# Attention with eight heads: the last head's projection weights fetched during the fourth head, from ScalarE's queue

## The chip, the cores and the metric

The kernel runs on one core of a Trainium2 chip. The metric is the device time of one launch in microseconds (us). Before the change it is 1582.3 us, the median of three runs (1581.09 to 1584.79). One further execution was taken with the hardware profiler; every row of the trace below is from it.

The engines are named as in the profile: PE is TensorE (matmuls; PEld its weight loads), DVE is VectorE, ACT is ScalarE, POOL is GpSimd, SP is SyncE, which does nothing but issue DMAs. SPq and ACTq are the rows in which SyncE and ScalarE issue one.

## The reference, cut to what matters

The reference is a whole decoder block. An RMS-normalised input feeds a state-space branch and an attention branch; both are gated and merged, and a cross-attention and a feed-forward layer follow. The change lies in the attention branch, which computes for each of 8 heads of width 64, over 1024 tokens:

```python
q, k, v = u @ w_in[:, 512:1024], u @ w_in[:, 1024:1536], u @ w_in[:, 1536:2048]
s = einsum('bhqd,bhkd->bhqk', q, k) * 64 ** -0.5 + cum[..., :, None] - cum[..., None, :]
p = softmax(where(causal, s, -inf))
out = einsum('bhqk,bhkd->bhqd', p, v)          # cum: running sum of log sigmoid(forget logit)
```

Of `w_in`, one head's projection needs 64 columns for q and 64 for k, 1024 rows each. The GLU that is spoken of below is the product of the state-space branch with `w_glu`; its first products are made beside the last head.

## The kernel before, in words

**Precision.** Every float32 operand of a matmul is split in two: ScalarE copies a rounded "hi" part (L178, in `split`), VectorE subtracts to get "lo" (L179). A product is three matmuls, hi·hi, hi·lo, lo·hi (L168, L169, L170, in `mm3`). A block of weights therefore passes through a DMA into a `raw` tile, a copy on ScalarE into `whi`, and a subtraction on VectorE into `wlo`.

**Slots.** The pool `wpool` gives `raw`, `whi` and `wlo` four slots each, and these are shared: by the value weights, the eight heads' projection weights, the GLU's weights (`wload`, L153, two DMAs of 256 KB for each block) and later ones.

**The heads.** `Fox.run` goes through the heads h = 0 to 7. A head has 12 units (query half, key tile), numbered 0 to 11. A unit computes a tile of scores (L1650, L1651 on TensorE), adds a causal mask where the tile lies on the diagonal (L1653, VectorE), takes the exponential (L1657, ScalarE; the instruction is kept as `self.exp`), splits it (L1662 and L1663, or L1659 and L1660), and products with the values follow one or two units later (L1675, L1676, L1682).

Between the units stand pieces of other heads' work, in lists by unit (`side[i]`), so that TensorE always has something to do:

- the projection of head h+2, matmul by matmul (`parts`), with its copies out of PSUM into the `hb` tiles (`evac`, L1592 to L1598);
- the row maxima of head h+1 (L1623 on TensorE, L1625 and L1628 on VectorE). `max_row` turns them (L1637, L1639) and sends them by DMA into row 68 of that head's queries (L1640). The first scores of head h+1 read that row;
- the split of the weights of head h+3 at unit 9 (`parted`, which calls `split`), placed behind the exponential of that unit;
- the load of the weights of head h+3 at unit 5 for h = 1 to 4 (`load`, L1570 and L1571): two DMAs of 256 KB in rows of 256 bytes, issued by SyncE, and placed behind `self.spread`, the DMA that spreads the row of reciprocal sums of head h−1 (L1697, in `finish`).

So the weights of head 7 are loaded and split in head 4. `finish` sends a row of sums away, inverts it (L1694, VectorE) and fetches it back spread over 64 partitions (L1693, L1695, L1697); `divide` multiplies by it after unit 4 of the next head, splits the result and stores it (L1703, L178, L179, L1709). `gate_rows` fetches two rows of decay sums into the `hb` tiles (L1605, L1606).

**What sets the order.** The source above gives priorities; a scheduler in the compiler orders each engine's instructions and places the waits. `behind(ins)` and `issue_after(ins)` add a tie: the instructions inside stand behind `ins` on its engine, without a semaphore. In the trace, instructions can therefore stand earlier than in the source: the GLU's loads, which are written in head 7 (`filler`), are issued by SyncE in head 4, and their splits follow the split of head 7's weights.

**Other loads on SyncE near the change.** In heads 5 and 6, `load_y` (L1728) brings 16 pieces of the state-space branch's result.

Of the kernel before, what the change touches and what calls it, by code (L numbers as in the profile page):

```python
# [24 lines left out]
NH = 8  # L25
# [24 lines left out]
C_U, C_Q, C_K, C_V, C_G = 0, 512, 1024, 1536, 2056  # L50
# [16 lines left out]
def f32(ap):  # L67
    return ap.bitcast(F32)
# [26 lines left out]
def weave(main, side, lead=0):  # L95

    n, m, done = len(main) - lead, len(side), 0
    for i, f in enumerate(main):
        f()
        want = m if i + 1 == len(main) else max(0, (i + 1 - lead) * m // max(n, 1))  # L100
        while done < want:
            side[done]()
            done += 1
# [986 lines left out]
class Glu:  # L1090
# [6 lines left out]
    def load(self, j):  # L1097
        pieces = [(512 * i, (4, P), self.w_glu[:, :, i * D + j * P:i * D + (j + 1) * P].rearrange("k p c -> p k c"))
                  for i in range(2)]
        self.w[j] = [t[:, :D].rearrange("p (k c) -> p k c", k=8) for t in self.B.wload(pieces, D)]  # L1100
# [348 lines left out]
class Fox:  # L1449
# [109 lines left out]
    def project(self, h):  # L1559

        B = self.B
        V, A, S = B.V, B.A, B.S
        K1, K2, Q1, Q2 = self.hb[h % 2]

        def load(behind=None):
            src = lambda c: self.w_in[:, c + h * DH:c + (h + 1) * DH].rearrange("(k p) c -> p k c", p=P)
            raw = self.raw[h] = B.wpool.tile([P, RAW], F32, tag="raw", bufs=4, name="raw")[:, :D]
            rv = raw.rearrange("p (k c) -> p k c", k=8)
            with B.behind(behind):
                S.dma_start(rv[:, :, 0:64], src(C_Q))  # L1570
                return S.dma_start(rv[:, :, 64:128], src(C_K))  # L1571

        def parted(behind=None):
            wh = B.wpool.tile([P, WSLOT], F32R, tag="whi", name="whi")[:, :D]
            wl = B.wpool.tile([P, WSLOT], F32R, tag="wlo", name="wlo")[:, :D]
            with B.behind(behind):
                B.split(wh, wl, self.raw.pop(h))
            self.pj[h] = [t.rearrange("p (k c) -> p k c", k=8) for t in (wh, wl)]

        def part(hf, k):  # L1580
            if k == 0:
                self.pj[h, hf] = B.bank("mm")
            wh, wl = self.pj[h]
            rh, rl = self.uT.rhs(k, hf)
            B.mm3(self.pj[h, hf], wh[:, k, :], wl[:, k, :], rh, rl, k == 0, k == 7)

        def evac(hf):
            if hf == 1 and h > 1:
                self.gate_rows(h)
            ps = self.pj.pop((h, hf))  # L1590
            cs = slice(512 * hf, 512 * hf + 512)
            A.activation(Q1[0:64, cs], ps[0:64, :], AF.Copy, scale=0.125)  # L1592
            A.copy(K1[0:64, cs], ps[64:128, :])
            V.scalar_tensor_tensor(out=Q2[64:128, cs], in0=ps[0:64, :], scalar=0.125, in1=f32(Q1[0:64, cs]),
                                   op0=ALU.mult, op1=ALU.subtract)
            V.tensor_sub(K2[0:64, cs], ps[64:128, :], f32(K1[0:64, cs]))
            A.activation(Q2[0:64, cs], ps[0:64, :], AF.Copy, scale=0.125)
            return A.copy(K2[64:128, cs], ps[64:128, :])  # L1598

        return Projection(load, parted, [lambda hf=hf, k=k: part(hf, k) for hf in range(2) for k in range(8)],  # L1600
                          [lambda: evac(0), lambda: evac(1)])

# [113 lines left out]
    def run(self, y_d, yT, aT, w_glu, w_d, filler):  # L1716
        B, fp, S = self.B, self.fp, self.B.S
        self.aT = aT
        self.prepare_v()
        for t in range(NT):  # L1720
            self.values_of_v(1, t)
        self.log_forget()
        self.setup()

        def load_y(k, h):

            for i, dst in enumerate(yT.rhs(k, h)):
                S.dma_start(f32(dst).rearrange("p (t c) -> p t c", t=4),  # L1728
                            y_d[k, i, 4 * h:4 * h + 4].rearrange("t p c -> p t c"))

        def load_att(k):
            for h in range(2):
                for i, dst in enumerate(aT.rhs(k, h)):
                    S.dma_start(f32(dst), self.att_d[i, k * P:(k + 1) * P, 512 * h:512 * h + 512])

        pro = [self.project(h) for h in range(NH)]
        for h in range(2):
            loaded = pro[h].load()
            pro[h].split()

        with B.tc.issue_after(loaded.ins):
            for k in range(4):
                S.dma_start(w_d[k].rearrange("(m g) c -> m g c", g=8),
                            w_glu[k * P:(k + 1) * P].rearrange("(g m) c -> m g c", m=16))
        for f in pro[0].parts[:8] + pro[0].evac[:1] + pro[0].parts[8:] + pro[0].evac[1:]:
            f()
        self.cumulate()
        for t in range(4):
            self.values_of_v(0, t)
        for h in range(2):  # L1750
            self.gate_rows(h)
        for f in pro[1].parts[:4]:
            f()
        weave(pro[1].parts[4:8] + pro[1].evac[:1] + pro[1].parts[8:], self.row_max(0))
        copied = pro[1].evac[1]()
        self.values_of_v(0, 4)
        self.max_row(0)
        pro[2].load()
        pro[2].split(copied)
        pro[3].load()  # L1760
        for t in range(5, 7):
            self.values_of_v(0, t)
        units = [(qc, kt) for qc in range(2) for kt in range(4 * qc + 4)]
        for h in range(NH):
            side = {i: [] for i in range(12)}
            late = h == NH - 2
            if late:
                for i, f in enumerate(pro[h + 1].parts[8:]):
                    side[i // 2].append(f)
                side[3].append(pro[h + 1].evac[1])  # L1770
            if h + 1 < NH:
                for i, f in enumerate(self.row_max(h + 1)):
                    side[(RSLOT_LATE if late else RSLOT)[i]].append(f)
                side[9].append(lambda: self.max_row(h + 1))
            if h + 2 < NH:
                n = 8 if h + 3 == NH else 16
                for i, f in enumerate(pro[h + 2].parts[:n]):
                    side[i if n == 8 else PSLOT[i]].append(f)
                side[9].append(pro[h + 2].evac[0])
                if n == 16:  # L1780
                    side[11].append(pro[h + 2].evac[1])
            if h + 3 < NH:
                side[9].append(lambda: pro[h + 3].split(self.exp))
            if h > 0 and h + 3 < NH:
                side[5].append(lambda: pro[h + 3].load(self.spread))
            if h == 0:
                side[0].append(lambda: self.values_of_v(0, 7))
            if late:
                for k in range(8):
                    side[4 + k].append(lambda k=k: load_y(k // 2, k % 2))  # L1790
            if h == NH - 1:
                for k in range(3):
                    side[6 + k].append(lambda k=k: load_att(k))
                for i, f in enumerate(filler):
                    side[i * 12 // len(filler)].append(f)
            for i, u in enumerate(units):
                self.scores(h, *u)
                for f in side[i]:
                    f()
                if len(self.hi_todo) > 2:  # L1800
                    self.values_hi()
                if len(self.lo_todo) > 1:
                    self.values_lo()
                if h and i == 4:
                    with B.tc.issue_after(self.mark.ins):
                        self.divide(h - 1)
        while self.hi_todo:
            self.values_hi()
        while self.lo_todo:
            self.values_lo()  # L1810
        self.divide(NH - 1)
# [29 lines left out]
```

## Time and profile before

| | |
|---|---|
| median of three runs | 1582.3 us |
| the profiled execution | 1584.62 us |
| its span, first to last instruction | 1582.9 us |
| TensorE busy | 1536.4 us, 97% of the span |
| VectorE busy | 1026.6 us, 65% |
| ScalarE busy | 658.3 us, 42% |
| mean granted clock of TensorE | 0.985 of full speed |
| bytes moved by DMA | 240.87 MB, 152 GB/s over the span |

Times in rows of the trace are microseconds from the start of the span. A row of a timeline gives start, duration, engine, source line, operation, output and inputs with their shapes, and in brackets the time for which the engine was idle before it and what ended that. `x2` is two instructions merged into one row. In the view by stretches, each engine has its busy time and in parentheses the number of its instructions.

### The profile page before, as it was taken

The page shows a single profiled execution, that of the slowest core. Times are in us where ns is not written, and L with a number is a line of the kernel's source. Part 1 is how long each engine was busy: PE and PEld are TensorE (multiplying, and loading weights), DVE is VectorE, ACT ScalarE, POOL GpSimd, SP SyncE. Part 2 cuts the span into 40 slices and gives each one's busy share as a digit, 9 for nine tenths or more (in the row PEclk, how much of TensorE's full clock was granted, in tenths as well). Part 3 has the DMA queues.
Part 4 walks back from the last instruction along what each step waited for, and adds up shares of the span by engine and source line. Part 5 has one row for each costly group of instructions (what it writes and reads, how often), then busy time and mean ns, then how long its engine had stood idle before and what let it go on. Part 6 is the DMA issues. An engine that isn't in the chain of part 4 may idle for free.

```text
span 1582.9 us, 20443 instructions
## 1 busy us (share of the span) xinstructions
PE 1536.4 (97%) x7313; PEld 1264.3 (80%) x7313; DVE 1026.6 (65%) x1822; ACT 658.3 (42%) x1177; POOL 266.8 (17%) x343
## 2 busy tenths in 40 slices
PE   7899999999999899999999999999999999999997
PEld 6688888898777678878888778888888888788886
DVE  6746545444788687685555687777777775566555
ACT  6422434422566553232335564333333333344342
POOL 3026653200212124110002200100000000001001
PEclk8899999999999899999999999999999999999999
DMA  8753466422123746367412186555544543897652
GB/s 294 151 105 100 131 118 138 111 103 30 26 45 59 203 121 199 109 206 248 138 45 76 54 282 236 172 165 162 159 160 156 162 147 129 269 392 228 192 160 107
DMA packets 197942, 240.87 MB, mean 152 GB/s; under 512 B 35448, under 2 KB 126488, under 8 KB 197328
## 3 DMA queue, kind: packets, MB, share of 16 engines
q1 hardware_dynamic: 190640, 222.79, 47.7%
q10 hardware_dynamic: 7200, 16.78, 2.8%
q8 instruction: 57, 0.93, 0.2%
q14 instruction: 45, 0.37, 0.1%
HBM read 165.60 MB, written 75.86 MB: 153 GB/s over the span
## 4 chain that ended last, share of the span: by engine, by line
PE 83%; DVE 6%; DMA 5%; ACT 3%; issue 1%; POOL 1%; SPq 0%; POOLq 0%; ACTq 0%; DVEq 0%
PE mm L873 15%; PE mm L168 8%; PE mm L170 8%; PE mm L169 8%; PE pv L873 7%; PE mm L1010 4%; PE sc L873 4%; PE sc L168 3%; PE sc L169 3%; PE sc L170 3%; PE sc L1010 3%; PE pv L1010 3%; PE misc L1010 1%; DMA raw<-in_w_in_dram 1%; PE mm L1623 1%
## 5 line engine op out<-in xcount | busy, mean ns | idle before, releaser
L178 ACT CAST whi<-raw 128x1024 fp32r<-128x1024 f32 (+2 forms) x124 | 115.8, 940 | 172.3 <-PE mm L873 44.0
L179 DVE TENSOR_TENSOR wlo<-raw,whi 128x1024 fp32r<-128x1024 f32 (+2 forms) x121 | 130.0, 1079 | 74.4 <-ACT whi L178 72.3
L168 PE MATMUL mm<-uh,whi 128*128 128x512 f32 x344 | 138.7, 403 | 2.4 <-ACT whi L178 2.3
L170 PE MATMUL mm<-uh,wlo 128*128 128x512 f32 x344 | 136.7, 398 | 0.5 <-DVE wlo L179 0.5
L179 DVE TENSOR_TENSOR ol<-or,oh 128x1024 fp32r<-128x1024 f32 x73 | 92.2, 1267 | 68.6 <-ACT oh L178 67.5
L169 PE MATMUL mm<-ul,whi 128*128 128x512 f32 x344 | 136.7, 397 | 0.0
L178 ACT CAST oh<-or 128x1024 fp32r<-128x1024 f32 x73 | 76.8, 1053 | 104.1 <-PE mm L1010 33.6
L905 POOL TENSOR_TENSOR g<-a,c 128x512 f32<-128x512 f32 x22 | 37.9, 1723 | 390.1 <-ACT a L904 371.0
L1660 POOL TENSOR_TENSOR pl<-pf,ph 128x512 fp32r<-128x512 f32 (+1 forms) x32 | 37.9, 1183 | 244.4 <-DVE ph L1659 174.5
L168 PEld LDWEIGHTS mm<-uh,whi 128*128 128x128 f32 x344 | 65.9, 192 | 14.9 <-ACT whi L178 2.7
L170 PEld LDWEIGHTS mm<-uh,wlo 128*128 128x128 f32 x344 | 65.8, 191 | 14.9 <-DVE wlo L179 1.5
L169 PEld LDWEIGHTS mm<-ul,whi 128*128 128x128 f32 x344 | 65.9, 192 | 11.2
L197 POOL TENSOR_TENSOR r<-ms,mhalf 128x1 f32<-128x1 f32 (+1 forms) x30 | 19.4, 649 | 307.3 <-DVE ms L193 279.9
L1657 ACT ACTIVATE pf<-sc 128x512 f32<-128x512 f32 (+1 forms) x96 | 46.4, 490 | 45.6 <-DVE sc L1653 29.9
L873 PE MATMUL pv<-S3h,we 128*128 128x512 f32 x176 | 58.1, 389 | 0.0
L1663 DVE TENSOR_TENSOR pl<-pf,ph 128x512 fp32r<-128x512 f32 (+2 forms) x64 | 36.2, 567 | 9.8 <-ACT ph L1662 9.0
L1126 POOL TENSOR_TENSOR sg<-sg,ga 128x512 f32<-128x512 f32 x16 | 29.7, 1881 | 73.5 <-DVE sg L1119 60.1
L1010 PE MATMUL mm<-ol,oh 128*128 128x512 f32 x106 | 41.2, 389 | 0.0
L1010 PE MATMUL mm<-oh,ol 128*128 128x512 f32 x106 | 41.2, 389 | 0.0
L1010 PE MATMUL mm<-oh 128*128 128x512 f32 x106 | 41.2, 389 | 0.0
L168 PE MATMUL sc<-uh,whi 128*128 128x512 f32 x104 | 40.8, 392 | 0.0
L168 PE MATMUL mm<-yh,whi 128*128 128x512 f32 x104 | 40.7, 392 | 0.0
(583 smaller groups left out, 4563.7 us busy)
## 6 DMA issues: line engine op xcount, KB each, us to landing
or<-c_d SPq DMA_DIRECT2D x77, 256.0 KB
raw<-in_w_in_dram SPq DMA_DIRECT2D x22, 512.0 KB
wo<-in_w_ffn_out_dram SPq DMA_DIRECT2D x22, 512.0 KB
c_d<-g SPq DMA_DIRECT2D x44, 256.0 KB
t_d<-wo SPq DMA_DIRECT2D x44, 256.0 KB
or<-t_d SPq DMA_DIRECT2D x44, 256.0 KB
raw<-in_w_ffn_in_dram SPq DMA_DIRECT2D x20, 512.0 KB
rawb<-in_w_ffn_in_dram SPq DMA_DIRECT2D x20, 512.0 KB
```

The costliest lines, as they stand in the source:

```text
L168: T.matmul(ps, lh, rh, start=first, stop=False)
L169: T.matmul(ps, lh, rl, start=False, stop=False)
L170: T.matmul(ps, ll, rh, start=False, stop=last)
L178: self.A.copy(hi, src)
L179: (self.G if pool_lo else self.V).tensor_sub(lo, src, f32(hi))
L873: T.matmul(ps, l_[:, k, :], r_, start=first and k == 0 and i == 0, stop=k == 3 and i == 2, skip_group_check=True)
L905: G.tensor_mul(g[:, 512:], a1, c1)
L1010: T.matmul(ps, l_[:, gi], r_[:, 512:], start=n < 3 and p == 0 and k == 0 or n == 7 and p == 0 and k == 0, stop=p == NP - 1 and k == 2, ski ...
L1126: self.B.G.tensor_mul(self.out[j][:, cs], self.out[j][:, cs], ga)
L1657: self.exp = A.activation(pf[:, off:], ps[:, off:], AF.Exp)
L1660: G.tensor_sub(pl[:, off:], pf[:, off:], f32(ph[:, off:]))
L1663: V.tensor_sub(pl[:, off:], pf[:, off:], f32(ph[:, off:]))
```

## The change

`load` gets a parameter that says which engine issues its two DMAs; SyncE stays the default. At unit 5, the load of head h+3 is now placed for h = 1 to 3 only (heads 4, 5 and 6). In head 3, at unit 8, the load of head 7 is added, issued by ScalarE and tied behind the exponential of that unit (`self.exp`, L1657). Everything else in the source is the same: the split of head 7's weights stays at unit 9 of head 4, and all sizes and buffers stay.

```diff
-        def load(behind=None):
+        def load(behind=None, queue=S):
             src = lambda c: self.w_in[:, c + h * DH:c + (h + 1) * DH].rearrange("(k p) c -> p k c", p=P)
             raw = self.raw[h] = B.wpool.tile([P, RAW], F32, tag="raw", bufs=4, name="raw")[:, :D]
             rv = raw.rearrange("p (k c) -> p k c", k=8)
             with B.behind(behind):
-                S.dma_start(rv[:, :, 0:64], src(C_Q))
-                return S.dma_start(rv[:, :, 64:128], src(C_K))
+                queue.dma_start(rv[:, :, 0:64], src(C_Q))
+                return queue.dma_start(rv[:, :, 64:128], src(C_K))
...
-            if h > 0 and h + 3 < NH:
+            if 0 < h < NH - 4:
                 side[5].append(lambda: pro[h + 3].load(self.spread))
+            if h == NH - 5:
+                side[8].append(lambda: pro[NH - 1].load(self.exp, B.A))
```

## The prediction

> **What bounds the kernel now.** The profile page comes first: which engine is busy, which one the chain of waits names, and where TensorE's granted clock falls.
>
> ```profile
> PE 1536.4 (97%) x7313; PEld 1264.3 (80%) x7313; DVE 1026.6 (65%) x1822; ACT 658.3 (42%) x1177; POOL 266.8 (17%) x343
> PEclk8899999999999899999999999999999999999999
> PE 83%; DVE 6%; DMA 5%; ACT 3%; issue 1%; POOL 1%; SPq 0%; POOLq 0%; ACTq 0%; DVEq 0%
> ```
>
> TensorE is the bound, so an edit pays only where it removes TensorE idle time or low clock. Behind the first two slices the clock shows one dip: the 14th of 40 (514 to 554 us), where the fifth head's attention lies (heads are counted 0 to 7 from here, so that is head 4). A head begins with its first scores, the L1650 matmul of 512 columns; in TensorE's timeline these stand at 469.9, 494.8, 526.6 and 551.3. The view of busy time by stretch for head 3, head 4 and head 5, then for the parts around the dip (columns: length, busy time of PE with its matmuls, PEld, DVE, ACT, POOL, then clock, DMA share, GB/s):
>
> ```profile
> 469.90:494.80 24.90, 24.87 (x123) 18.90 (x123) 20.30 (x51) 16.86 (x33) 4.60 (x4) 1.00 0.32 54
> 494.80:526.60 31.80, 28.02 (x123) 20.19 (x122) 23.45 (x53) 19.26 (x36) 4.61 (x4) 0.88 0.46 101
> 526.60:551.30 24.70, 22.74 (x107) 16.81 (x106) 18.89 (x52) 14.29 (x28) 4.63 (x4) 0.94 0.85 219
> ...
> 515.80:519.20 3.40, 1.11 (x5) 0.39 (x3) 0.60 (x1) 1.49 (x3) 0.00 (x0) 1.00 0.97 282
> 519.20:529.40 10.20, 8.75 (x25) 6.34 (x25) 7.12 (x12) 7.71 (x14) 0.00 (x0) 0.50 0.42 121
> ```
>
> Heads 3 and 4 hold the same 123 matmuls, yet head 4 takes 6.9 us more. What ends its idle time is in the timelines of ScalarE, TensorE and VectorE; the last bracket is the idle time before an instruction and its releaser:
>
> ```profile
> 488.32 1.05 ACT L178 CAST whi<-raw 128x1024 fp32r<-128x1024 f32 x1
> ...
> 512.54 0.58 ACT L1598 CAST hb<-mm 64x512 fp32r<-64x512 f32 x1
> 517.52 1.04 ACT L178 CAST whi<-raw 128x1024 fp32r<-128x1024 f32 x1 [4.40 <-DMA raw<-in_w_in_dram]
> ...
> 494.79 0.39 PE L1650 MATMUL sc<-hb 69*128 69x512 f32 x1
> ...
> 518.62 0.50 PE L168 MATMUL mm<-uh,whi 128*128 128x512 f32 x1 [2.29 <-ACT whi L178]
> 519.88 0.79 PE L170 MATMUL mm<-uh,wlo 128*128 128x512 f32 x1 [0.53 <-DVE wlo L179]
> 523.75 0.37 PE L1675 MATMUL pv<-ph,vhi 128*65 128x128 f32 x1 [0.92 <-ACT ph L1662]
> ```
>
> Head 3 splits head 6's weights at 488.32 without a wait. Head 4 reaches the split of head 7's weights at 513.12 (512.54 + 0.58) and sits for 4.40 us until the DMA has landed. TensorE runs dry for 2.29 us, and right behind the stretch in which it worked 1.11 of 3.40 us its clock is 0.50 for 10.2 us. Why the load is late is in SyncE's timeline: head 3's load of weights, then head 4's, then what follows.
>
> ```profile
> 477.38 0.58 SPq L1571 DMA_DIRECT2D raw<-in_w_in_dram  x1
> 490.98 0.70 SPq L1640 DMA_DIRECT2D hb<-mr  x1
> ...
> 499.57 0.35 SPq L1695 DMA_DIRECT2D rd_d<-rc  x1
> 501.00 0.46 SPq L1697 DMA_DIRECT2D rb<-rd_d  x1
> 501.52 0.58 SPq L1570 DMA_DIRECT2D raw<-in_w_in_dram  x1
> 502.15 0.57 SPq L1571 DMA_DIRECT2D raw<-in_w_in_dram  x1
> 502.77 8.01 SPq L153 DMA_DIRECT2D raw<-wg_d  x2
> 510.88 3.11 SPq L1709 DMA_DIRECT2D att_d<-ahi  x1
> 514.08 0.67 SPq L1709 DMA_DIRECT2D att_d<-alo  x1
> 514.80 3.63 SPq L153 DMA_DIRECT2D raw<-wg_d  x4
> ```
>
> Head 3's load was through by the time of its split, at most 10.9 us after its second issue (477.38 to 488.32); head 4's took 15.4 us (502.15 to 517.52). Only behind head 4's load do six loads of the GLU's weights follow (L153).
>
> **The change part by part.**
>
> *Removed:* the two loads on SyncE at 501.52. *Added:* the same two on ScalarE in head 3, behind the exponential of unit 8.
>
> ```profile
> 485.76 0.98 ACT L1657 ACTIVATE pf<-sc 128x512 f32<-128x512 f32 x2 [0.77 <-DVE sc L1653]
> 487.20 0.50 ACT L1662 CAST ph<-pf 128x384 fp32r<-128x384 f32 x1
> 490.77 0.35 PE L1675 MATMUL pv<-ph,vhi 128*65 128x384 f32 x1
> ```
>
> The row of 485.76 is units 8 and 9, so the loads go out near 486.3. With the slow 15.4 us they land by 502, and the split needs them at 513.12: **the 4.40 us go**, with 11 us to spare. The buffer is the one that head 3's weights left, split in head 0, so no wait comes with it.
>
> What goes with the wait: head 4's excess over head 3, 31.80 − 24.90 = **6.9 us**, which holds all three idle pieces and the half clock up to 526.6; and in head 5 the rest of the half clock, 526.6 to 529.4, 2.8 us at 0.50, so **1.4 us**. Sum 8.3 us.
>
> *Late next:* the splits of three GLU blocks, which in before fall into the disturbed end of head 4. They cannot move ahead of head 7's split, since they take their slots after it.
>
> ```profile
> 519.14 1.05 ACT L178 CAST whi<-raw 128x1024 fp32r<-128x1024 f32 x1 [0.17 <-DMA raw<-wg_d]
> 521.81 1.04 ACT L178 CAST whi<-raw 128x1024 fp32r<-128x1024 f32 x1 [1.32 <-DMA raw<-wg_d]
> 524.21 1.04 ACT L178 CAST whi<-raw 128x1024 fp32r<-128x1024 f32 x1
> 525.66 1.21 DVE L179 TENSOR_TENSOR wlo<-raw,whi 128x1024 fp32r<-128x1024 f32 x1
> 492.19 0.68 DVE L1594 SCALAR_TENSOR_TENSOR hb<-mm,hb 64x512 fp32r<-64x512 f32 x1 [0.63 <-ACT hb L1593]
> 495.45 0.65 DVE L1653 TENSOR_TENSOR sc<-sc,trk 128x128 f32<-128x128 f32 x2 [1.53 <-PE sc L1651]
> ```
>
> On VectorE they cost 3 x 1.21 = 3.6 us. At the same place of head 3, VectorE was idle for 0.63 + 1.53 = 2.2 us. So between 0 (TensorE has other products queued) and 3.6 − 2.2 = 1.4 us reaches TensorE; I take **0.8**, a little over the middle, since ScalarE carries 3.1 us of the same splits.
>
> *ScalarE's two issues.* No row shows this transfer issued from ScalarE. From below, its stores of the gates took 0.33 us each; from above, SyncE's third and fourth such load in a row:
>
> ```profile
> L475 ACTq DMA_DIRECT2D gate_d<-gs x32: 326/326/348, 113.8 to 316.8; - x32
> 360.62 1.21 SPq L1570 DMA_DIRECT2D raw<-in_w_in_dram  x1
> 361.87 3.43 SPq L1571 DMA_DIRECT2D raw<-in_w_in_dram  x1
> ```
>
> That is 0.7 to 4.6 us for both. I take SyncE's pair of head 4, 0.58 + 0.57 = 1.2 us, being the same transfer with no load ahead of it. Behind it waits unit 9's exponential, whose cast now ends at 487.70 and is used at 490.77: 3.1 us of cover, so **0**. At 4.6 us the cover is short by 1.5 us.
>
> The Trainium skill (DMA: Bandwidth & Descriptors, "Issuing engines are not separate DMA queues") says that DMAs issued from several engines run on the same 16 DMA engines and interleave, and that only issue time is saved. By that the other queue alone would gain nothing; the sum rests on the earlier issue, which the rule leaves as it is.
>
> *SyncE's queue.* Three rows above stand back to back: 501.52, 502.15, 502.77. The GLU's loads are head 7's work in the source and two of the four slots were free before; they come the moment head 7's slot is taken. I read that as slots being given out in source order. So the first two blocks will now go out near 486.5 as well, about 4 us ahead of the row of maxima (L1640, 490.98) that head 4's first scores need at 494.79. Bounds: nothing, if that row still lands by 494.79; 6.0 us of TensorE idle at the worst (rival 2). I take **0**: DMA share was 0.08 from 486 to 497, and the four rows issued at 514.80 were off SyncE in 3.63 us even behind a full queue.
>
> ```profile
> 486.00:497.00 11.00, 10.97 (x57) 8.32 (x56) 8.06 (x20) 8.26 (x17) 1.28 (x1) 1.00 0.08 16
> ```
>
> **Sum:** 6.9 + 1.4 − 0.8 − 0 − 0 = **7.5 us**. From the profiled run's own 1584.62 us (span 1582.9) that gives 1577.1; that run lies 2.3 us above the median of the three, 1582.3, from which it gives **1574.8**. Heads 5 to 7 and the tail follow from head 4's end by waits, so the gain is handed on.
>
> **The rivals.**
>
> 1. *The clock does not come back.* If the half clock has another cause than the stall, 10.2 us at half speed (5.1 us) stay and the gain is 7.5 − 5.1 = 2.4 us: 1579.9. Against it stands a second place:
>
> ```profile
> 372.40:375.85 3.45, 2.31 (x8) 1.43 (x9) 2.20 (x8) 0.76 (x2) 0.00 (x0) 1.00 0.26 41
> 375.85:379.27 3.42, 3.42 (x10) 2.67 (x9) 1.62 (x6) 0.00 (x0) 0.00 (x0) 0.50 0.00 0
> ```
>
> There 1.14 us of idle in 3.45 were followed by half clock too. The Trainium skill (TensorE: Matmul & The Clock Gate, "What's actually happening") has the clock fall after an idle window of about 3.4 us; by that a stall of 2.29 us is too short and this rival would hold. Both places of the trace speak against it. Chance 0.05.
>
> 2. *The stall moves to the start of head 4, slower.* All six GLU loads get ahead of the row of maxima. Held as in head 4 (8.01 + 3.63 = 11.6 us) from 486.5, SyncE issues that row at 498.1; with 0.7 us of issue and some 2 us to land (an estimate: the store of rc issued at 499.57 let the next DMA go at 501.00), TensorE idles from 494.8 to 500.8, 6.0 us, and pays the half clock of 5.1 us again: 11.1 − 7.5 = 3.6 us **slower**, 1585.9. It decides above 7.5 − 5.1 = 2.4 us of idle. For it: the two behind head 4's load did hold SyncE for 8.01 us. Against: head 7's 512 KB will not stand ahead of them on this queue. Chance 0.13.
>
> 3. *The same at smaller size.* ScalarE's issue at 4.6 us, or the row of maxima 1 to 3 us late: 1.5 to 3 us of idle and a half clock of 3.4 to 10.2 us (1.7 to 5.1 us lost), together 3.2 to 8.1: 1578.0 to 1582.9, 1580.5 in the middle. Chance 0.17; a third of it is still faster by over 0.2%.
>
> 4. *Nothing changes*, the loads being placed as late as before: 1582.3. The tie to unit 8 speaks against. Chance 0.03.
>
> **How the numbers follow.** Forecast 0.62, and its own range 1572.5 to 1577.5: 8.3 us of gain at most gives 1574.0, and the runs of before reach 1.2 us below and 2.5 above their median. About 0.2% (3.2 us) is what a measurement here can tell from no change. Faster: 0.62 + 0.06 (of rival 3) = 0.68, and 0.02 for rival 1's better half: 0.70. Same: 0.03 + 0.11 + 0.03 = 0.17. Slower: 0.13. The range reaches from 1572.5 to 1584.0; left out are rival 2 and some of both edges.
>
> **What would show it.** Right: no wait of ScalarE's L178 for in_w_in_dram; head 4 about 25.7 us long with its 123 matmuls; clock 1.00 from 496 to 545; GLU loads on SyncE from about 486. The 0.8 us shows as idle of TensorE between head 7's split and head 5's first scores. Wrong: TensorE waiting at L1650 near 494.8 or a clock of 0.50 anywhere from 486 to 530; two issues on ScalarE over 3 us.

## The result and the profile after

After the change the kernel takes **1592.24 us** (median of 6 runs, 1590.93 to 1596.98), and before, in the runs beside it, 1583.76 us (6 runs, 1581.09 to 1586.46). The ratio is 1.0055, with a 95% interval of 1.0041 to 1.0070: **slower by about 8.5 us**, where 1574.8 us was forecast. The profiled spans differ by 1589.2 − 1582.9 = 6.3 us.

The page of after: the clock row has its dip one slice earlier, in the 13th of 40.

```profile
PE 1532.4 (96%) x7313; PEld 1261.9 (79%) x7313; DVE 1024.1 (64%) x1822; ACT 658.2 (41%) x1177; POOL 264.6 (17%) x343
PEclk8999999999998999999999999999999999999999
```

Busy time by stretch, from one head's first scores to the next head's, for heads 3 to 6 of after, then the idle piece at head 4's start and the stretch at half clock (columns as in the prediction):

```profile
469.63:503.41 33.78, 21.97 (x107) 16.26 (x105) 18.35 (x48) 15.67 (x31) 4.59 (x4) 0.90 0.54 92
503.41:532.63 29.22, 29.22 (x137) 22.38 (x138) 23.63 (x54) 20.00 (x36) 5.50 (x4) 0.94 0.17 43
532.63:557.36 24.73, 21.87 (x107) 15.74 (x106) 20.27 (x54) 14.76 (x29) 4.62 (x4) 1.00 0.89 224
557.36:580.40 23.04, 21.85 (x106) 15.50 (x104) 19.66 (x46) 14.36 (x29) 4.61 (x4) 1.00 0.49 134
491.63:503.41 11.78, 0.00 (x1) 0.03 (x1) 1.00 (x2) 0.83 (x3) 0.00 (x0) 0.71 0.64 119
496.60:506.80 10.20, 3.39 (x9) 2.63 (x10) 2.10 (x5) 1.32 (x3) 0.00 (x0) 0.50 0.60 143
```

The same stretches of before, cut in the same way:

```profile
469.96:494.79 24.83, 24.80 (x122) 18.88 (x121) 20.30 (x51) 16.79 (x33) 4.60 (x4) 1.00 0.32 55
494.79:526.59 31.80, 28.02 (x122) 20.19 (x121) 23.44 (x53) 19.26 (x36) 4.61 (x4) 0.88 0.46 101
526.59:551.28 24.69, 22.73 (x107) 16.79 (x105) 18.90 (x52) 14.30 (x28) 4.63 (x4) 0.94 0.85 219
551.28:574.36 23.08, 21.89 (x105) 15.51 (x104) 19.67 (x46) 14.36 (x29) 4.63 (x4) 1.00 0.48 132
```

Head 3 is 8.95 us longer, head 4 is 2.58 us shorter, heads 5 and 6 are as they were: 6.37 us, the whole difference of the spans. Head 3 also holds 15 matmuls fewer, which head 4 does instead.

ScalarE's timeline of after answers to the rows of the wait that was to go:

```profile
485.45 0.43 ACTq L1570 DMA_DIRECT2D raw<-in_w_in_dram  x1
485.92 0.86 ACTq L1571 DMA_DIRECT2D raw<-in_w_in_dram  x1
486.83 0.49 ACT L1657 ACTIVATE pf<-sc 128x384 f32<-128x384 f32 x1 [0.81 <-DVE ph L1659]
...
526.32 1.05 ACT L178 CAST whi<-raw 128x1024 fp32r<-128x1024 f32 x1
```

The two issues take 1.29 us and head 7's split (526.32) waits for nothing. TensorE's timeline shows what took the place of that wait, SyncE's what was on the way, and the chain of waits names one piece:

```profile
491.23 0.40 PE L169 MATMUL mm<-ul,whi 128*128 128x512 f32 x1
503.41 0.77 PE L1650 MATMUL sc<-hb 69*128 69x512 f32 x1 [11.78 <-DMA hb<-mr]
```

```profile
484.58 7.03 SPq L153 DMA_DIRECT2D raw<-wg_d  x4
491.71 2.31 SPq L1640 DMA_DIRECT2D hb<-mr  x1
```

```profile
491.71 11.56 DMA hb<-mr
```

TensorE stands for 11.78 us for the row of maxima, a DMA of 4 KB that is issued at 491.71 and not there before 503.4. Four loads of the GLU's weights went out ahead of it on SyncE, and head 7's load runs beside it on ScalarE's queue.

### The profile page after: what moved, and what is told of

The parts are those of the page before. It is cut to its first block, busy times and chain, and to the rows that moved or that the text cites. A ratio compares the mean times of both kernels' runs of the same rounds, so it can differ in the third digit from the quotient of the medians.

```text
span 1589.2 us, 20444 instructions
## 1 busy us (share of the span) xinstructions
PE 1532.4 (96%) x7313; PEld 1261.9 (79%) x7313; DVE 1024.1 (64%) x1822; ACT 658.2 (41%) x1177; POOL 264.6 (17%) x343
## 4 chain that ended last, share of the span: by engine, by line
PE 81%; DVE 7%; DMA 6%; ACT 3%; POOL 2%; issue 2%; SPq 0%; POOLq 0%; ACTq 0%; DVEq 0%
PE mm L873 15%; PE mm L168 8%; PE mm L170 8%; PE mm L169 8%; PE pv L873 7%; PE mm L1010 5%; PE sc L873 4%; PE sc L1010 4%; PE sc L168 3%; PE sc L170 3%; PE sc L169 3%; PE pv L1010 3%; PE misc L1010 2%; DMA raw<-in_w_in_dram 1%; DMA raw<-in_w_mem_kv_dram 1%
## 5 line engine op out<-in xcount | busy, mean ns | idle before, releaser
L169 PEld LDWEIGHTS mm<-ul,whi 128*128 128x128 f32 x344 | 65.2, 190 | 11.2
L1657 ACT ACTIVATE pf<-sc 128x512 f32<-128x512 f32 (+1 forms) x96 | 46.4, 489 | 57.6 <-DVE sc L1653 39.2
```

The source lines that it names most:

```text
L169: T.matmul(ps, lh, rl, start=False, stop=False)
L1657: self.exp = A.activation(pf[:, off:], ps[:, off:], AF.Exp)
```

## The experiments

**Theories.** A: SyncE's order is to blame, since the GLU's loads stand ahead of the row of maxima. B: two queues at once disturb each other, whatever they carry. C: head 7's load is slow wherever it is put, and DMAs issued while it runs land only when it is through. C comes from two stretches of before, behind head 3's load and behind head 4's, which moved 123 and 33 GB/s:

```profile
478.00:484.20 6.20, 6.20 (x31) 4.60 (x31) 5.30 (x9) 4.47 (x7) 1.47 (x2) 1.00 0.80 123
503.00:511.00 8.00, 8.00 (x40) 5.95 (x39) 7.02 (x15) 5.29 (x9) 1.30 (x2) 1.00 0.40 33
```

**e1: the GLU's loads tied behind head 4's spread DMA (L1697).** Only SyncE's order differs from after; `wload` (L153) gets `held`, for which `Glu.load` passes `B.hold`.

```diff
+            with self.behind(held): self.S.dma_start(...)
-                self.scores(h, *u)
+                self.scores(h, *u); B.hold = self.spread if (h, i) == (4, 5) else B.hold
```

> The changed kernel with one thing different: the six GLU loads on SyncE are tied behind the DMA of the reciprocal sums in head 4 (L1697), where they stood before the change. Every other engine has the changed kernel's order. Theory A (SyncE's order: the four GLU loads that now stand ahead of the row of maxima, L1640, hold it up): L1640 is issued near 489.6 instead of 491.7, lands within about 2 us, TensorE waits at most 1 us for head 4's first scores (11.8 us in the changed kernel), there is no half clock there, and the time is 1576 to 1579 (before 1583 on the mean of its runs). Theory B (two queues at once: ScalarE's load of 256-byte rows starves whatever SyncE issues meanwhile): the row of maxima, issued while that load runs, still lands late, at 495 to 500, TensorE idles 4 to 8 us, and the time is 1584 to 1590.

Measured: 1592.79 us against 1584.74, ratio 1.0047 (1.0031 to 1.0062). SyncE's timeline, TensorE's, and the DMA queues from 488 to 497 and then from 497 to 503 (packets, MB, share of 16 engines; q1 is what SyncE issued, q10 what ScalarE did):

```profile
484.98 0.46 SPq L1709 DMA_DIRECT2D att_d<-alo  x1
490.45 0.70 SPq L1640 DMA_DIRECT2D hb<-mr  x1
491.25 2.12 SPq L1605 DMA_DIRECT2D hb<-cum_d  x1
```

```profile
502.50 0.77 PE L1650 MATMUL sc<-hb 69*128 69x512 f32 x1 [9.96 <-DMA hb<-mr]
```

```profile
q10 hardware_dynamic: 960, 0.24, 46.1%
```

```profile
q10 hardware_dynamic: 1067, 0.27, 28.6%
q1 hardware_dynamic: 24, 0.02, 1.0%
```

Nothing stands ahead of the row on SyncE for 5 us, and it is still 12.05 us from its issue to the first scores. From 488 to 497 the DMA engines carry 960 packets of head 7's load and not one of SyncE's, although three of its DMAs wait (the second fetch of decay sums follows at 493.42). Between 500 and 502 the last 406 packets of the load and the last 8 of SyncE's 24 move, and the first scores start at 502.50. So the GLU's loads are not needed for the wait, and theory A falls as its cause; holding them back took 1.8 us off it (11.78 to 9.96). B had expected 4 to 8 us of idle and 1584 to 1590 us, both too little.

**e2: the GLU's loads tied behind head 3's row of maxima instead.** `B.hold` is set to that DMA at head 3, unit 10.

> The changed kernel, with the six GLU loads tied behind head 3's row of maxima (L1640): they stay in head 3 but go out after it. Theory A: like e1 for the start of head 4, 1576 to 1580; the GLU loads then run beside the fetch of head 3's reciprocal sums, which may cost 1 to 2 us. Theory B: L1640 late as in e1, 1584 to 1590.

Measured: 1593.19 us, ratio 1.0049 (1.0029 to 1.0069); TensorE waits 9.80 us at the same place. The same as e1, and again more than B's 1584 to 1590 us.

**e3 and e4: head 7's load from SyncE, behind head 2's last store; e4 also holds the GLU's loads as e1 does.**

```diff
-                side[8].append(lambda: pro[NH - 1].load(self.exp, B.A))
+                side[8].append(lambda: pro[NH - 1].load(self.stored))
```

> Head 7's weights loaded in head 3 as in the change, but from SyncE, tied behind head 2's last store (L1709); of the GLU loads one now stands ahead of the row of maxima, the rest behind it. Theory A: the row stands behind 512 KB of head 7 and 256 KB of the GLU on one queue and lands 5 to 12 us late: 1584 to 1592. Theory B (only the second queue does the harm): no late row, 1576 to 1580. A third theory C (this load is slow wherever it is put, about 15 us, and whatever is issued behind or beside it waits for it): late as in theory A, landing near 500, 1588 to 1594.

> As e3, and the GLU loads held to head 4 as in e1: ahead of the row of maxima stands head 7's load alone, on the same queue. Theory A (the GLU loads are the harm): the load takes the 7 us that head 6's took, is through by 492, and the time is 1576 to 1579. Theory C: the load takes 15 us, the row of maxima lands near 500, TensorE idles 5 to 8 us: 1586 to 1591.

Measured: e3 1586.94 us, ratio 1.0016 (1.0006 to 1.0026), a wait of 6.95 us; e4 1584.77 us, ratio 0.9999 (0.9985 to 1.0013). Both lie below what C gave (1588 to 1594 and 1586 to 1591). SyncE's timeline of e4, then TensorE's:

```profile
482.69 0.58 SPq L1570 DMA_DIRECT2D raw<-in_w_in_dram  x1
...
490.08 1.96 SPq L1640 DMA_DIRECT2D hb<-mr  x1
```

```profile
497.19 0.79 PE L1650 MATMUL sc<-hb 69*128 69x512 f32 x1 [4.51 <-DMA hb<-mr]
```

The wait is there from one queue too, 5.45 us shorter than in e1. Counted from head 3's start (467.71 in e4, 470.47 in e1), TensorE comes to the scores 2.90 us later, the load is issued 0.91 us earlier, and from its issue to the scores pass 14.50 us against 16.14. B in its plain form, that it takes two queues, falls.

**e5: before, with the columns of heads 6 and 7 exchanged.**

```diff
-            src = lambda c: self.w_in[...]
+            src = lambda c, h=h ^ (h > 5): self.w_in[...]
```

> The kernel before, with the columns of heads 6 and 7 exchanged in the loads: the load issued near 477 fetches head 7's columns, the one near 501 head 6's (so these two heads' attention is computed with the other's weights). Theory C in the form that the columns are slow: the first 1024 rows of 256 bytes of the load at 477 come at about 100 in a us, the load lands at 491 to 493, ScalarE waits 3 to 5 us for it at 488 and the row of maxima of head 3 is late too; the load at 501 lands by 510 and ScalarE's wait of 4.4 us at 513 is gone; the stall stands one head earlier and the time is 1582 to 1590. In the form that the place is slow (the slot, the time in the program, what runs beside it): nothing changes, the wait stays at 513 and the time is that of before.

Measured: 1582.0 us, ratio 0.9982 (0.9967 to 0.9996). The stretches of e5 behind the issue in head 3, which now fetches head 7's columns, and behind the issue in head 4; then ScalarE's timeline at head 3's split:

```profile
474.70:484.70 10.00, 10.00 (x48) 7.42 (x47) 8.72 (x17) 7.18 (x13) 2.39 (x3) 1.00 0.46 53
502.00:509.00 7.00, 7.00 (x35) 5.28 (x34) 5.52 (x11) 4.92 (x8) 2.53 (x2) 1.00 0.84 132
```

```profile
489.57 1.04 ACT L178 CAST whi<-raw 128x1024 fp32r<-128x1024 f32 x1 [3.87 <-DMA raw<-in_w_in_dram]
```

The 53 GB/s stand where before had 123, the 132 where it had 33. The wait has moved with the columns: 3.87 us at head 3's split, where before had none, and none at head 4's. The row of maxima, which I had expected late as well, was not: it was issued at 492.09, behind the load's end, and head 4's first scores do not wait. The slowness belongs to the columns, not to the place, the slot or the neighbours.

**e6: the eight loads alone,** one after the other, three turns with other slots, the third from ScalarE; all else is left out.

> Only the loads of the eight heads' projection weights, a pair of DMAs for each head, one pair after the other, nothing else running (the rest of the block is left out): first with head h in slot h mod 4, from SyncE, then in slot (h + 1) mod 4, from SyncE, then as at first from ScalarE. If the columns are slow by themselves, head 7's pair takes 13 to 15 us in all three turns and the others about 7; if the slot is slow, head 3's and 7's pairs are slow in the first and third turn and head 2's and 6's in the second; if only the company of other work is slow, all pairs take about 7 us or less.

Measured: 243.14 us. VectorE touches each pair of loads as it lands; the bracket is the wait. The first two heads of turn one, then the first head of turns two and three:

```profile
17.41 0.17 DVE L83 COPY raw<-raw 128x2 f32<-128x2 f32 x1 [11.73 <-DMA raw<-in_w_in_dram]
24.92 0.17 DVE L83 COPY raw<-raw 128x2 f32<-128x2 f32 x1 [7.33 <-DMA raw<-in_w_in_dram]
...
92.66 0.17 DVE L83 COPY raw<-raw 128x2 f32<-128x2 f32 x1 [14.25 <-DMA raw<-in_w_in_dram]
...
167.66 0.17 DVE L83 COPY raw<-raw 128x2 f32<-128x2 f32 x1 [13.82 <-DMA raw<-in_w_in_dram]
```

One head is slow by itself, in the two slots that it had and from either queue, with nothing beside it. Here it is head 0, not head 7, so the matrix's columns alone do not decide; e13 goes on from there.

**e8: before, with the GLU's loads tied behind head 4's row of maxima,** so that none follows head 7's load on SyncE.

> The kernel before, with the GLU loads tied behind head 4's row of maxima (they then come after head 5's), so that nothing follows head 7's load on SyncE until two stores. If the GLU loads behind it made head 7's load slow, it now takes 7 us, lands by 510, and the time is 1576 to 1580 (less what the later GLU loads cost). If it is slow by itself, it lands at 515 to 517, ScalarE still waits 2 to 4 us and the time is 1582 to 1590.

Measured: 1582.31 us, ratio 0.9987 (0.9975 to 1.0). ScalarE's split of head 7's weights still waits 3.09 us: the load isn't late because of what follows it.

**e9, e10, e11: the turn of head 7 loads head 5's columns,** in after (e9), in e1 (e10) and in before (e11).

```diff
+            src = lambda c, h=5 if h == 7 else h: self.w_in[...]
```

> The kernel after, but the turn of head 7 loads the columns of head 5, so the slow columns are not loaded in the fourth head; the result of head 7 is another head's. Place, queue, bytes and the GLU loads on SyncE are those of after. Theory C (these columns are slow wherever they are loaded, and what is issued beside them waits): the load takes 5 to 8 us instead of some 13, the wait for the row of maxima falls from 11.8 us to 0 to 4 us, 1576 to 1585 us. Theory A (the GLU loads ahead of the row on SyncE): the same 7.0 us of issue ahead of it, so 9 to 12 us of wait, 1590 to 1593 us. Theory B (two queues at once): as A, 1590 to 1593 us.

> The kernel of e1 (GLU loads held behind head 4's spread DMA) with the columns of head 5 in the turn of head 7. Nothing stands ahead of the row of maxima on SyncE. C: the row lands in time, idle under 2 us, no half clock at the start of head 4, 1574 to 1580 us, which is what the prediction had. B: the load on the other queue still blocks, 8 to 10 us of idle as in e1, 1590 us or more.

> The kernel before with the columns of head 5 in the turn of head 7. C: the load issued near 501.5 lands by 509 and the wait of 4.40 us at the split goes, with the half clock behind it: 6 to 8 us less, 1576 to 1579 us. If the two GLU loads behind it on the queue were the reason for its 15.4 us: the wait stays and the time is that of before, 1582 to 1585 us.

**e12 and e7: head 7's weights loaded in head 0,** from SyncE behind head 0's row of maxima; e7 also holds the GLU's loads.

```diff
-            if h == NH - 5:
-                side[8].append(lambda: pro[NH - 1].load(self.exp, B.A))
+            if h == 0:
+                side[1].append(lambda: pro[NH - 1].load(self.rowed))
```

> The kernel of e7 (head 7's weights loaded in head 0) without the hold on the GLU loads, which then go out ahead of head 4's row of maxima on SyncE, as in after. C: without a slow load beside it the row comes at most 2 to 4 us late: 1578 to 1584 us, near e7. A: the GLU loads ahead of the row cost by themselves 6 us or more of idle and the half clock: 1587 to 1592 us.

> Head 7's weights are loaded in head 0 instead, from SyncE, behind head 0's row of maxima, where no other load of weights stands in the program and about 20 us pass until SyncE's next small DMA; the GLU loads are held to head 4 as in e1. If the load is slow wherever it is put but nothing is behind it here, no row of maxima is late, ScalarE's wait of 4.4 us is gone, the clock stays at 1.00 from 496 to 530 and the time is 6 to 8 us under before: 1576 to 1579. If the gain that was forecast does not exist, it is within 2 us of before.

The row of maxima on SyncE and TensorE's first scores of head 4, in e9, then in e10, then in e12 with the GLU's loads:

```profile
491.81 1.49 SPq L1640 DMA_DIRECT2D hb<-mr  x1
...
499.12 0.76 PE L1650 MATMUL sc<-hb 69*128 69x512 f32 x1 [6.86 <-DMA hb<-mr]
```

```profile
487.88 0.70 SPq L1640 DMA_DIRECT2D hb<-mr  x1
...
492.18 0.47 PE L1650 MATMUL sc<-hb 69*128 69x512 f32 x1 [2.23 <-DMA hb<-mr]
```

```profile
477.96 4.86 SPq L153 DMA_DIRECT2D raw<-wg_d  x2
...
485.95 2.15 SPq L153 DMA_DIRECT2D raw<-wg_d  x2
...
491.00 0.71 SPq L1640 DMA_DIRECT2D hb<-mr  x1
...
494.80 0.39 PE L1650 MATMUL sc<-hb 69*128 69x512 f32 x1
```

| kernel | load beside the row of maxima | GLU loads ahead of it | its issue to first scores, us | TensorE waits, us | ratio to before |
|---|---|---|---|---|---|
| after | head 7's columns | 4, directly | 491.71 to 503.41: 11.7 | 11.78 | 1.0055 (1.0041 to 1.0070) |
| e1 | head 7's columns | none | 490.45 to 502.50: 12.1 | 9.96 | 1.0047 (1.0031 to 1.0062) |
| e9 | head 5's columns | 4, directly | 491.81 to 499.12: 7.3 | 6.86 | 1.0022 (1.0010 to 1.0035) |
| e10 | head 5's columns | none | 487.88 to 492.18: 4.3 | 2.23 | 0.9977 (0.9961 to 0.9994) |
| e12 | none | 2 from 13 us, 2 from 5 us ahead | 491.00 to 494.80: 3.8 or less | 0 | 0.9963 (0.9944 to 0.9981) |

The fourth column is the one to compare, since e12 has more cover: its TensorE comes to the scores 24.86 us into head 3, as in before, and the other four come 22.0 to 22.1 us into it. The row of maxima takes 3.8 us at most with no load beside it (e12), 4.3 with a load of ordinary columns beside it (e10), 7.3 with the GLU's loads directly ahead of it as well (e9), 12.1 with the slow columns alone (e1). So an ordinary load beside the row costs little (e10's 2.23 us are less than the lost cover), and the slow columns add 7.8 us to the row's time (e1 against e10), or 4.4 with the GLU's loads ahead (after against e9). In e10 too the row waits for the load: of SyncE's 24 packets 19 move between 490 and 492, together with the load's last 702, and from 492 to 494 none of either queue.

C holds, but not as I wrote it. For e9 I expected 0 to 4 us of wait and 1576 to 1585 us; it was 6.86 and 1588.26, and neither A nor B gives that either (9 to 12 us). For e10 I expected under 2 us, no half clock and at most 1580 us; it was 2.23, a clock of 0.60 from 493.5 to 497.0, and 1580.7. What the GLU's loads cost is not settled: those of e12 did no harm, but the last of them was off SyncE 2.9 us before the row, while in after and e9 the row follows them at once. No kernel has them directly ahead of the row without a load beside it.

e11 gives 1579.0 us, ratio 0.9960 (0.9944 to 0.9976): the wait that the change set out to remove goes when nothing is moved and only the slow columns aren't read. Stretches of e11 for heads 3 to 5:

```profile
468.30:493.09 24.79, 24.76 (x122) 18.87 (x121) 20.22 (x51) 16.77 (x33) 4.60 (x4) 1.00 0.32 55
493.09:518.06 24.97, 24.84 (x122) 18.66 (x121) 21.89 (x52) 18.44 (x35) 4.61 (x4) 1.00 0.52 124
518.06:542.47 24.41, 21.85 (x107) 15.77 (x106) 19.99 (x53) 14.89 (x29) 4.62 (x4) 1.00 0.88 228
```

**e7 beats both kernels:** 1578.9 us (7 runs, 1574.55 to 1581.14) against 1585.02, ratio 0.9963 (0.9949 to 0.9977). e12, the same without the hold, has 1579.91 against 1584.92 and the same ratio. Stretches of e7: the load in head 0, and head 4.

```profile
389.50:399.50 10.00, 10.00 (x62) 8.52 (x62) 5.88 (x17) 4.98 (x10) 0.74 (x1) 1.00 0.41 31
...
496.11:521.13 25.02, 24.79 (x123) 18.70 (x122) 21.61 (x51) 18.70 (x35) 4.59 (x4) 1.00 0.42 99
```

The load is as slow as ever, 31 GB/s, but starts right behind one row of maxima (388.04) and is through long before the next (414.73). Head 4 takes 25.0 us.

**e13 and e14: a map of the columns.** Loads of 64 columns, 1024 rows each, one after the other, over 64 blocks, twice, in one run each; e14 gives each partition eight neighbouring rows in place of rows 128 apart. All else is left out.

> Only loads of 64 columns of the input projection (1024 packets of 256 B each), one after the other from SyncE, for all 64 column blocks of the first 4096 columns, twice; everything else is left out. Theory C in its strongest form (a few column blocks are slow, the same ones each time): most blocks take 4 to 6 us from one issue to the next, a few take 9 to 13 us, and the same blocks in both turns. Rival (the slowness is an effect of what ran just before or of a refresh-like event): slow blocks at other places in the second turn. If the offset within 4096 or 2048 bytes decides, the slow blocks stand at a fixed distance of 16 or 8 blocks.

> The loads of e13 (1024 rows of 64 columns, all column blocks twice), with another share of rows for a partition: partition p gets the eight neighbouring rows 8p to 8p+7 instead of the rows p, p+128, ... p+896. Same bytes, same packets of 256 B, other order. In e13 the eight rows of a partition lie 128 x 16416 B = 513 x 4096 B apart, at the same place within 4096 B, and one block in 16 (one place in 4096 B) takes 11.2 us instead of 4.4 to 7.7. If that spacing is what makes the block slow: here all blocks take about the same, 4 to 7 us, and none over 9. If the column's place in 4096 B decides by itself: one block in 16 stays above 9 us.

VectorE's waits in e13, in the first turn and at the ninth block of the second, then in e14:

```profile
55.10 0.17 DVE L83 COPY raw<-raw 128x2 f32<-128x2 f32 x1 [9.21 <-DMA raw<-in_w_in_dram]
66.48 0.17 DVE L83 COPY raw<-raw 128x2 f32<-128x2 f32 x1 [11.21 <-DMA raw<-in_w_in_dram]
73.02 0.17 DVE L83 COPY raw<-raw 128x2 f32<-128x2 f32 x1 [6.37 <-DMA raw<-in_w_in_dram]
...
174.16 0.17 DVE L83 COPY raw<-raw 128x2 f32<-128x2 f32 x1 [11.20 <-DMA raw<-in_w_in_dram]
...
493.24 0.17 DVE L83 COPY raw<-raw 128x2 f32<-128x2 f32 x1 [11.17 <-DMA raw<-in_w_in_dram]
```

```profile
65.89 0.17 DVE L83 COPY raw<-raw 128x2 f32<-128x2 f32 x1 [11.60 <-DMA raw<-in_w_in_dram]
...
171.78 0.17 DVE L83 COPY raw<-raw 128x2 f32<-128x2 f32 x1 [11.57 <-DMA raw<-in_w_in_dram]
```

Exactly one block in 16 is slow, the ninth, in all eight groups of 16 of the two turns; VectorE waits 11.2 to 11.9 us for it, for the others 4.0 to 9.4 but for the very first block (3.3) and a single 10.2 in the second turn. Sixteen blocks of 256 bytes are 4096 bytes: **the columns' offset, counted modulo 4096 bytes, decides.** It is a matter of degree: the block before the slow one takes 8.2 to 9.4 us in all eight groups. Nor is one place in memory slow: rows are 16416 = 4 x 4096 + 32 bytes apart, so the rows of any block start at 128 places within 4096 bytes, the same 128 for every block. The ninth block is head 0's q columns, which agrees with e6; in the whole kernel it is head 7's. That the matrix lies at another offset there would explain the shift, but its address wasn't looked at. The spacing of a partition's rows does not matter (e14), against my expectation. Why that one offset is slow stays open.

## Why the prediction was wrong, point by point

- *"The 4.40 us go":* right. No wait at head 7's split.
- *ScalarE's two issues, "0":* right. 0.43 + 0.86 = 1.29 us against 1.2, and no wait behind them.
- *What goes with the wait, 8.3 us, less 0.8 for the GLU's splits:* somewhat too high. In e11 head 4 falls from 31.80 to 24.97 us, 6.83, so the splits cost about 0.2 (24.97 against that kernel's head 3, 24.79). But head 5 gains only 0.28 of the 1.4 us: its busy time falls by 0.88 (22.73 to 21.85), and its idle time grows from 1.96 to 2.56. In whole times the wait is worth 5.9 us (1584.92 − 1579.0).
- ***"SyncE's queue. [...] I take 0"* is the step that failed.** The reading that the GLU's loads would go out ahead of the row was right (484.58), and they were not the main price: without them, in e1, 9.96 of the 11.78 us of wait remain. What I priced wrongly, at 0, is the transfer itself. I had its 15.4 us and asked only whether it would land by 513; I did not ask which small DMA, due at 494.79, would be under way in those 15.4 us. The argument that the DMA share was 0.08 from 486 to 497 is drawn from a profile in which the load is not yet there.
- *Rival 2* had the place and the sign, but its mechanism was SyncE's issue time, 6.0 us. "Against: head 7's 512 KB will not stand ahead of them on this queue" is the sentence that e1 refutes: on the other queue it stood in the way all the same. The wait was 11.78 us.
- *Not in any step:* the scheduler put head 4's first scores earlier. TensorE was ready for them 22.00 us into head 3 (491.63 − 469.63), in before 24.83. The 2.83 us of cover were gone, and the 15 matmuls that had given it ran later. This goes with the issue from ScalarE: e1, e2, e9 and e10 have it as well (22.0 to 22.1 us), while e3 and e4, with the load on SyncE in the same head, come at 25.0 us.
- *The clock follows the stall* (rival 1 falls): 10.2 us at 0.50, as priced. But only 3.39 us of busy time lie in it, 1.7 us lost instead of 5.1, since TensorE idled through the rest anyway.

The corrected sum: head 3 + 11.78 − 2.83 = + 8.95; head 4 − 6.83 (the old wait) + 2.83 (the matmuls that moved) + 1.70 (half clock) = − 2.30, measured − 2.58. Together + 6.65 against + 6.37 in the spans.

The Trainium skill (DMA: Bandwidth & Descriptors, "Issuing engines are not separate DMA queues") spoke against a gain from the other queue: transfers from several engines share the DMA engines, and another issuing engine saves only issue time. I weighed it for what the change would gain, not for what it would cost. e1 agrees that the queue gave no room of its own, but it does not show the interleaving that the section speaks of: 960 packets of one queue and none of the other in 9 us. In after, where SyncE issued the GLU's loads at the same time, both queues moved: 30 packets of SyncE's beside 744 of ScalarE's from 488 to 495 us, and 366 beside 1105 if the count goes on to 497.

## What to carry to other kernels

Before moving a large transfer, list the small DMAs that become due while it runs, on every queue, and put their due times against its end: another issuing engine does not keep them apart, and a free DMA share in the old profile says nothing of the new one. Put such a transfer right behind the last urgent row, with its whole length free before the next, as e7 did. When one of several equal transfers is slow, exchange what they read (e5) before blaming its neighbours.

## What the runs showed of the hardware

- **A column block can be slow by its offset.** Loads of 1024 rows of 256 bytes took 11.2 to 11.9 us for one block in 16 and 4.0 to 9.4 us for nearly all others (e13), with a period of 4096 bytes in the column offset, with nothing else under way. The Trainium skill (DMA: Bandwidth & Descriptors, "Latency and other measured facts") tells of copies that slow down at row pitches of large powers of two; these rows are 16416 bytes apart, and another spacing per partition changed nothing (e14), so that rule does not account for it.
- **A DMA of 4 KB was not there for 12.1 us beside another queue's load,** with nothing ahead of it on its own for 5 us (e1); without such a load it took 3.8 us at most (e12). Its wait ended with that load's last packets (e1, e10).
- **Half clock fell on time that was idle anyway:** 6.8 of its 10.2 us in after.
